# A hybrid decoder layer: the feed-forward stages' first chunk pair in seven products instead of eight

## The chip, the core and the metric

The program runs on one core of one Trainium2 chip. The time is device microseconds of one execution, from the start of the program to its end. Five engines work beside each other, each through its own list of instructions: PE (matrix multiply, with PEld for its weight loads), DVE (vector), ACT (scalar), POOL (GpSimd) and SP. SP computes nothing here: it issues the weight loads. POOL issues transfers too, among them the accumulating ones, which add what they read onto what stands in the on-chip memory.

## The reference

One decoder layer for 256 tokens of width 2048, in fp32: a SwiGLU feed-forward half step, a token mixer, another feed-forward half step, each followed by a layer norm of the sum with a scaled residual.

```python
def _swiglu(x, w_gate, w_up, w_down):
    return (jax.nn.silu(x @ w_gate) * (x @ w_up)) @ w_down

h = _layer_norm(ALPHA * h + 0.5 * _swiglu(h, ffn1_w_gate, ffn1_w_up, ffn1_w_down), ln1_g, ln1_b)
mix = _mixer(h, positions, ...)            # latent attention, differential attention, gates
h = _layer_norm(ALPHA * h + mix, ln2_g, ln2_b)
h = _layer_norm(ALPHA * h + 0.5 * _swiglu(h, ffn2_w_gate, ffn2_w_up, ffn2_w_down), ln3_g, ln3_b)
```

The feed-forward width is 5632. The change is about `x @ w_gate` and `x @ w_up`, in both feed-forward stages.

## The kernel before

**Tiles.** Tokens are two blocks of 128 (b = 0, 1). The width 2048 is 16 k tiles of 128, in four quads of four. Gate and up weights are stored interleaved, in 22 chunks of 512 columns (256 of gate, 256 of up). A chunk's weights come in eight pieces of two k tiles, 128x1024, half a megabyte each (`raw`, four buffers). A product is a matmul of 128 tokens with 128x512 weights.

**Splitting.** PE multiplies numbers in a short form (fp32r). So every operand is split into a high part (a cast on ACT, L154) and a low part (a subtraction on DVE, L155), and each product is three matmuls, high by high, high by low, low by high (`triple`, L208 to L210). The split weights go into a ring of six pairs (`wring`).

**Plain form and seven products.** `project` computes a chunk in plain form: 16 k tiles, two token blocks, three matmuls, 96 a chunk, 192 a pair of chunks. `Hybrid.group` takes a pair of chunks and multiplies part of the k tiles by a scheme with seven products in place of eight: the operands are blocks 11, 12, 21, 22 of weights (first or second chunk of the pair as the second figure, first or second half of the k tiles concerned as the first) and sums of them, and sums of x (`Seven`: `fa`, `fb`, `minus`, `as_is`, whose split forms are `xs`). In `wide` groups each of the seven products has five k tiles (the fifth comes from `Extra`, `xe`, `xm` and the half pieces `eraw`), and three of eight pieces a chunk stay plain: 7 x 15 + 72 = 177 matmuls a pair. A weight sum is formed in two ways: by DVE (block 22 added to 11, then 21 to 11, L451), or by POOL with an accumulating transfer of block 12 onto 11 and onto 22 (L453, L458). Product 5 needs 11 + 12, so it waits for the transfer that is issued once product 1 has split 11.

**Order.** A string gives the order of units: a digit is a product, `p` and `q` a plain piece of the first and second chunk, `n` the next pair's product 1. Units go through a pipeline of load, split and multiply, three and four units deep; `later(n, f)` runs f n units on. The instructions of each engine are then put in order at build time by a scheduler that counts on its own estimates of durations; `issue_after` holds an instruction behind another on the same engine. On the chip each engine follows its list. A load waits for its buffer, and SP's later loads stand behind it.

**A feed-forward stage before the change:** pair 0 by `project` twice (chunk 0, chunk 1, x being loaded or, in stage two, normalised meanwhile), then pairs 1 to 10 by `Hybrid`, pair 1 with its product 1 as the first unit and Y seeded only from pair 2 on. In stage two pair 1's blocks are loaded early, in `second`. Then comes the down projection, in which `setup` makes the mixer's constants (mask, biases, sines), 70 units after the layer norm object is made.

Of the kernel before, what the change touches and what calls it, by code (L numbers as in the profile page):

```python
# [59 lines left out]
def layer_kernel(ctx: ExitStack, tc: tile.TileContext, a: dict, out: bass.AP):  # L60
# [55 lines left out]
    class Acts:  # L116
        def __init__(self, k, name, kept=()):
            self.name = name
            self.kept = kept
            self.tiles = {}  # L120
            self.ready = set()
            self.made = {}
            self.cast = {}
            self.raws = {}
# [13 lines left out]
        def put(self, q, b, src, i0=0, n=4):  # L138
            hi, lo = self.quad(q, b)
# [126 lines left out]
    class Seven:  # L266


        def __init__(self, raws, order=None, plain=None):

            self.raws, self.order, self.plain = raws, order, plain
            self.at_ = {}
            self.steps = [self.sums, lambda: self.pair(self.fa, 5, 6), lambda: self.pair(self.fb, 7, 3),
                          self.as_is, self.minus]

# [80 lines left out]
    class Hybrid:  # L356


        def __init__(self, x, seven, k_tiles, small=False, extra=None, early=()):
# [3 lines left out]
            self.early = set(early)  # L363
            names = ("11", "12", "22", "21") if small else ("11", "22", "21", "other 11")
            self.raws = {n: early[n] if n in early else [act_tile([P, 1024], F32, "sraw") for _ in range(2)] for n in names}
            self.shared = False
            if extra is not None:
                for pair in (("11", "22"), ("21", "other 11")):
                    t = act_tile([P, 2, 512], F32, "eraw")
                    for i, n in enumerate(pair):  # L370
                        self.raws[n] = self.raws[n] + [t[:, i, :]]
            self.snaps = [act_tile([P, 2, 512], F32, "snap") for _ in range(2)]

# [4 lines left out]
        def run(self, groups):  # L378

            parts = []  # L380
            for g in groups:
                parts.append(self.group(*g[:-1]))
                self.raws["11"], self.raws["other 11"] = self.raws["other 11"], self.raws["11"]
            for i, (order, emit) in enumerate(parts):
                groups[i][-1]()
                for c in order if i == 0 else order[1:]:
                    if c != "n":
                        emit(c)
                    elif i + 1 < len(parts):
                        parts[i + 1][1]("1")  # L390

        def group(self, w0, w1, done, wide=False, seeded=False, gates=False):
# [4 lines left out]
            there, self.early = self.early, ()  # L397
# [37 lines left out]
            def seventh(p, s):  # L435
# [4 lines left out]
                def load():  # L440
                    if s < 2 and load_block in there:
                        return
                    nc.sync.dma_start(R[load_block][s], source(load_block, s))
# [256 lines left out]
    def rows_to_quad(src, b, x, q, gain=None, shift=None, shared=False):  # L700
# [3 lines left out]
        if gain is not None:  # L704
            full = x.raw(q, b) if q in x.kept else tmp_tile([P, 512], "full")
            if shared and q % 2 == 1:
                v, o = (u.rearrange("p (i t) -> p i t", i=4) for u in (full, t))
                g, b0 = (u[:, 4 * q:4 * q + 4].unsqueeze(2).to_broadcast([P, 4, P]) for u in (gain, shift))
                with tc.issue_after(x.made[q - 3, b].ins) if q > 2 else nullcontext():
                    V.tensor_tensor(out=v, in0=o, in1=g, op=ALU.mult)  # L710
# [60 lines left out]
    class LayerNorm:  # L771
# [109 lines left out]
        def apply(self, b):  # L881
# [42 lines left out]
            for c in range(4):  # L924
# [4 lines left out]
            for c in range(4):  # L929
                later((12 if self.ahead is None else 10 + 4 * b) + c, lambda c=c: self.each(b, c, zs[c]))  # L930

    def ffn(n, x, wgu, wdn, residual, g, bt, each, first=None, between=None, nxt=None, cols=None, norm=None, pending=None):
# [7 lines left out]
        def half(c, b, up, gate, wait=0, single=False):  # L940
            q = c // 2
            sg = tmp_tile([P, 256], "sg")
            with tc.issue_after(weights[0][0].ins) if single else nullcontext():
                S.activation(sg, gate, AF.Silu)
            if c % 2 == 0:
# [3 lines left out]
            def product():  # L949
                with tc.issue_after(weights[0][1].ins) if single else behind_split(3) if wait else nullcontext():  # L950
# [5 lines left out]
            if c % 2 == 1:  # L956
                later(12, lambda: put_h(b, q))

        def gu_done(c, b, bank):
            if c == 0:  # L960
                later(3, lambda: half(c, b, bank[:, 256:512], bank[:, 0:256], 1, True))
            else:
                half(c, b, bank[:, 256:512], bank[:, 0:256])

        def sum_done(c, b, bank, snap, op):
            if snap is None:
                gu_done(c, b, bank)
# [30 lines left out]
        early = {}  # L998

        def second(j):  # L1000
            if j == (6 if norm is None else 0):
# [3 lines left out]
            if norm is not None and j in (0, 2, 4):  # L1005
                name, w, j0 = (("11", 2, 0), ("22", 3, 2), ("21", 2, 2))[j // 2]
                early[name] = [act_tile([P, 1024], F32, "sraw") for _ in range(2)]
                for s in range(2):
                    nc.sync.dma_start(early[name][s], wgu[w][j0 + s])

        def first_hook(j):
            if first is not None:
                first(j)
            if j == 5:
                for i, f in enumerate([extra.make] + seven.steps):
                    later(2 * i + 1 - (i > 0), f)
# [5 lines left out]
        def ask():  # L1022
            for i, q in enumerate((3, 4, 0)):
                for b in range(2):
                    later(1 + 4 * i + 2 * b, lambda q=q, b=b: get_half(q, b))
            later(13, lambda: split_h(3))
            later(16, lambda: split_h(4))
        hy.run([(wgu[2 * p], wgu[2 * p + 1],
                 lambda n, b, bank, snap, op, p=p: sum_done(2 * p + n, b, bank, snap, op),
                 True, p > 1, ask if p == KF // 4 - 1 else lambda: None)  # L1030
                for p in range(1, KF // 4)])
# [3 lines left out]
        if n == 1:  # L1035
            later(70, setup)
# [444 lines left out]
    xq = Acts(KD, "x", (0, 1, 2))  # L1481
# [6 lines left out]
    def first_tokens(j):  # L1488
        if j % 2 == 0:
            load_x(j // 2, 0)  # L1490

    def second_tokens(j):
        if j % 2 == 0:
            load_x(j // 2, 1)
# [9 lines left out]
    ffn(1, xq, a["gu1"], a["dn1"], a["x"], a["ln1_g"], a["ln1_b"], keep(0), first_tokens, second_tokens, h1, a["ln1_cols"])  # L1504
# [3 lines left out]
    h2 = Acts(KD, "h2", (0, 1, 2))  # L1508
# [96 lines left out]
```

## Time and profile before

| | |
|---|---|
| median of 3 runs | 1982.29 us (1978.77 to 1983.79) |
| the profiled execution's own time | 1982.59 us |
| its span, first to last instruction | 1980.8 us |
| PE busy | 1960.7 us, 99% |
| DVE busy | 1743.7 us, 88% |
| ACT busy | 1269.4 us, 64% |
| granted TensorE clock, mean | 0.996 |

Rows of the views are read like this. A timeline row is start, duration, engine, line, operation, result<-operands, shape and count, in us from the span's start; a bracket behind it gives the engine's idle time before it and what ended that. A windows row is a stretch, its length, then busy time and instruction count of PE, PEld, DVE, ACT and POOL, the granted TensorE clock (1.00 is full), the busy share of the DMA engines and GB/s. A DMA row is the transfer, the queue's engine, count, size and median us from issue to landing. A matmul's duration of 0.39 us overlaps the next one's.

### The profile page before, as it was taken

The page shows a single profiled execution, that of the slowest core. Times are in us where ns is not written, and L with a number is a line of the kernel's source. Part 1 is how long each engine was busy: PE and PEld are TensorE (multiplying, and loading weights), DVE is VectorE, ACT ScalarE, POOL GpSimd, SP SyncE. Part 2 cuts the span into 40 slices and gives each one's busy share as a digit, 9 for nine tenths or more (in the row PEclk, how much of TensorE's full clock was granted, in tenths as well). Part 3 has the DMA queues.
Part 4 walks back from the last instruction along what each step waited for, and adds up shares of the span by engine and source line. Part 5 has one row for each costly group of instructions (what it writes and reads, how often), then busy time and mean ns, then how long its engine had stood idle before and what let it go on. Part 6 is the DMA issues. An engine that isn't in the chain of part 4 may idle for free. (4 is left out here: it accounts for less than half of the span.)

```text
span 1980.8 us, 25910 instructions
## 1 busy us (share of the span) xinstructions
PE 1960.7 (99%) x8751; PEld 1617.2 (82%) x8751; DVE 1743.7 (88%) x2161; ACT 1269.4 (64%) x1660; POOL 367.8 (19%) x600
## 2 busy tenths in 40 slices
PE   9899999999999999999999999999999999999998
PEld 8788888888878888888888888887888888888886
DVE  7799999999898879999987777779999999999997
ACT  6567766676656576666667655556767667766662
POOL 0112221222100010102241530011222123210000
PEclk9999999999999999999999999999999999999999
DMA  8888888787867657668686798688888878887773
GB/s 308 257 258 227 248 276 275 223 257 258 302 211 247 196 187 296 232 213 255 214 255 202 228 303 275 204 274 246 235 252 284 265 221 245 264 323 242 275 233 125
DMA packets 151958, 489.93 MB, mean 247 GB/s; under 512 B 21984, under 2 KB 22288, under 8 KB 151824
## 3 DMA queue, kind: packets, MB, share of 16 engines
q1 hardware_dynamic: 111744, 374.78, 53.4%
q0 software_dynamic: 39936, 113.35, 24.0%
q8 instruction: 68, 1.11, 0.2%
q14 instruction: 66, 0.54, 0.1%
q10 hardware_dynamic: 144, 0.13, 0.0%
HBM read 457.77 MB, written 30.41 MB: 246 GB/s over the span
## 5 line engine op out<-in xcount | busy, mean ns | idle before, releaser
L154 ACT CAST wring<-raw 128x1024 fp32r<-128x1024 f32 (+2 forms) x460 | 474.1, 1035 | 298.9 <-PE mm L210 211.7
L155 DVE TENSOR_TENSOR wring<-raw,wring 128x1024 fp32r<-128x1024 f32 (+2 forms) x460 | 545.4, 1198 | 111.0 <-ACT wring L154 108.7
L154 ACT CAST wring<-sraw 128x1024 fp32r<-128x1024 f32 x436 | 456.2, 1052 | 175.7 <-PE mm L210 67.4
L155 DVE TENSOR_TENSOR wring<-sraw,wring 128x1024 fp32r<-128x1024 f32 x436 | 524.5, 1217 | 47.8 <-ACT wring L154 43.7
L208 PE MATMUL mm<-wring,h 128*128 128x512 f32 (+2 forms) x1176 | 454.4, 386 | 0.0
L209 PE MATMUL mm<-wring,h 128*128 128x512 f32 (+2 forms) x1176 | 452.4, 385 | 0.4 <-DVE wring L155 0.4
L210 PE MATMUL mm<-wring,h 128*128 128x512 f32 (+2 forms) x1176 | 452.6, 385 | 0.0
L208 PEld LDWEIGHTS mm<-wring,h 128*128 128x128 f32 x1176 | 221.2, 188 | 47.0 <-ACT snap L409 3.3
L209 PEld LDWEIGHTS mm<-wring,h 128*128 128x128 f32 x1176 | 221.1, 188 | 44.1 <-DVE wring L155 1.1
L210 PEld LDWEIGHTS mm<-wring,h 128*128 128x128 f32 x1176 | 221.1, 188 | 43.8 <-DVE h L155 0.9
L209 PE MATMUL mm<-wring,xs 128*128 128x512 f32 x616 | 239.9, 390 | 0.2 <-DVE wring L155 0.2
L208 PE MATMUL mm<-wring,xs 128*128 128x512 f32 x616 | 240.1, 390 | 0.0
L210 PE MATMUL mm<-wring,xs 128*128 128x512 f32 x616 | 239.7, 389 | 0.0
L451 DVE TENSOR_TENSOR sraw<-sraw,sraw 128x1024 f32<-128x1024 f32 x128 | 153.7, 1217 | 1.2 <-DMA sraw<-in_wgm_dram 0.7
L209 PEld LDWEIGHTS mm<-wring,xs 128*128 128x128 f32 x616 | 115.7, 188 | 25.1 <-DVE wring L155 1.0
L210 PEld LDWEIGHTS mm<-wring,xs 128*128 128x128 f32 x616 | 115.6, 188 | 24.1
L208 PEld LDWEIGHTS mm<-wring,xs 128*128 128x128 f32 x616 | 115.6, 188 | 24.1
L749 POOL DMA_DIRECT2D hT<-blocks x176 | 98.4, 575 | 182.5 <-DVE blocks L747 94.8
L453 POOL DMA_DIRECT2D sraw<-in_gu_dram x40 | 35.1, 885 | 435.4 <-DVE sraw L451 410.5
L208 PE MATMUL mm<-wring,x 128*128 128x512 f32 x264 | 103.8, 396 | 0.4 <-ACT wring L154 0.4
L209 PE MATMUL mm<-wring,x 128*128 128x512 f32 x264 | 103.4, 392 | 0.2 <-DVE wring L155 0.2
L210 PE MATMUL mm<-wring,x 128*128 128x512 f32 x264 | 103.3, 391 | 0.0
(350 smaller groups left out, 2876.7 us busy)
## 6 DMA issues: line engine op xcount, KB each, us to landing
raw<-in_gu_dram SPq DMA_DIRECT2D x150, 512.0 KB, 6.3
raw<-in_dn_dram SPq DMA_DIRECT2D x140, 512.0 KB, 4.6
sraw<-in_gu_dram SPq DMA_DIRECT2D x120, 512.0 KB, 6.7
sraw<-in_gu_dram POOLq DMA_DIRECT2D x80, 512.0 KB, 7.0
sraw<-in_dn_dram SPq DMA_DIRECT2D x36, 512.0 KB, 5.7
raw<-in_w_out_dram SPq DMA_DIRECT2D x32, 512.0 KB, 4.4
eraw<-in_gu_dram SPq DMA_DIRECT2D x60, 256.0 KB, 6.9
hraw<-hT POOLq DMA_DIRECT2D x56, 256.0 KB, 5.1
```

The lines of the kernel that those rows point to most:

```text
L154: cast[0] = S.copy(hi, src)
L155: lows[0] = V.tensor_tensor(out=lo, in0=src, in1=hi.bitcast(F32), op=ALU.subtract)
L208: PE.matmul(o, xh, wh, start=first, stop=False, skip_group_check=again)
L209: PE.matmul(o, xh, wl, start=False, stop=False, skip_group_check=again)
L210: PE.matmul(o, xl, wh, start=False, stop=last, skip_group_check=again)
L451: last = V.tensor_tensor(out=R[src][i], in0=R[src][i], in1=R[add[1]][i], op=ALU.add)
L453: nc.gpsimd.dma_start(R["22"][s], source("12", s), accum_op=ALU.add)
L749: nc.gpsimd.dma_start(to.rearrange("(g r) (i f) -> i r g f", g=4, i=4)[i], t[32 * i:32 * (i + 1), :].rearrange("r (g f) -> r g f", g=4))
```

## The change

In both feed-forward stages pair 0 is computed by a new method, `Hybrid.opening`, with the order `pqp1qpqp536n2q74`. k tiles 0 to 7 go through the seven products with four k tiles each (no fifth), k tiles 8 to 15 stay plain, four pieces a chunk. Seven of the eight plain pieces are put in the order ahead of product 5. Products 1, 6 and 7 share a bank A in turn, product 5 has a bank D; their sums are kept in `snap` and added at the end. Product 1 of pair 1 stands inside the opening, at `n`, and pair 1 is seeded like the later ones.

Quads 0 and 1 of x (the `formed` ones) are no longer split as they are; they enter only in the forms. The quads are loaded, and in stage two normalised, in the order 2, 3, 0, 1. `run` now starts each group when it is reached. The early loads of pair 1's blocks in stage two are gone. `setup` is traced 84 units after the layer norm object instead of 70, which is 14 units further on. The layer norm's writes of its result to memory come earlier in the count of units.

```diff
+        def opening(self, w0, w1, done, order, hook, guard, settle):
+            plan = {1: ("11", "11", None, "A"), 5: (None, "11", None, "D"), 6: (None, "11", "22", "A"),
+                    7: (None, "22", None, "A"), 2: ("21", "21", None, "Y"), 4: (None, "11", "21", "W"),
+                    3: ("22", "22", None, "Z")}
...
+                def prep():
+                    t = block(src)[s]
+                    last = None
+                    if add is not None:
+                        with behind_split(s + 1):
+                            last = V.tensor_tensor(out=t, in0=t, in1=block(add)[s], op=ALU.add)
+                    pair = next_pair()
+                    with guard(u), tc.issue_after(last.ins) if last is not None else nullcontext():
+                        split_in_line(True, *pair, t)
+                    if p in (1, 6):
+                        nc.gpsimd.dma_start(block("11" if p == 1 else "22")[s], w1[s], accum_op=ALU.add)
...
+            def plain(u, n, j):
...
+                def prep():
+                    pair = next_pair()
+                    with guard(u):
+                        for c in parts:
+                            split_in_line(u > 8, *(t[:, c] for t in pair), st["raw"][:, c])
...
-        project(wgu[0], x, KD, 512, lambda b, bank: gu_done(0, b, bank), hook=first_hook,
-                between=between, norm=norm)
-        project(wgu[1], x, KD, 512, lambda b, bank: gu_done(1, b, bank), hook=second, norm=norm, free=(0, 0))
-        look(3, 4)
-        hy = Hybrid(x, seven, KD, extra=extra, early=early)
...
+            def begin():
+                if p == 0:
+                    return hy.opening(wgu[0], wgu[1], done, "pqp1qpqp536n2q74", first, guard, settle)
+                return hy.group(wgu[2 * p], wgu[2 * p + 1], done, True, True)
...
-            later(70, setup)
+            later(84, setup)
...
-    xq = Acts(KD, "x", (0, 1, 2))
+    xq = Acts(KD, "x", (0, 1, 2), (0, 1))
...
-    h2 = Acts(KD, "h2", (0, 1, 2))
+    h2 = Acts(KD, "h2", (0, 1, 2), (0, 1))
```

How this moves the instructions is seen in the engines' lists. The names: `raw` is a plain piece, `sraw` and `eraw` are block pieces, `xs` a split form of x, `sg` the gate's activation, `snap` a kept sum; DMAHW stands for a transfer that SP issued, DMASW for one of POOL's, mostly an accumulating one.

ACT, stage one, where product 5 is first cast. Before, this is pair 1's product 5 (sraw_83, sraw_84 and eraw_91 are block 11):

```order
L154 CAST wring_14_114<-raw_95_478 128x1024 [waits DMAHW2_49,DVE_49,PE_49]
L944 ACTIVATE sg_81_454<-mm_59_317 128x256 [waits PE_49]
L154 CAST wring_4_104<-sraw_83_463 128x1024 [waits DMASW0_49,DVE_49,PE_49]
L154 CAST wring_20_120<-eraw_91_471 128x512 [waits DMASW2_49,DVE_49,PE_49]
L944 ACTIVATE sg_98_508<-mm_60_324 128x256 [waits PE_49]
L154 CAST wring_2_102<-sraw_84_464 128x1024 [waits DMASW1_49]
```

Now it is pair 0's (sraw_36 and sraw_37 are block 11; raw_42, raw_41, raw_44 and raw_47 are plain pieces, in the order in which PE takes them):

```order
L158 CAST wring_20_120<-raw_42_222 128x1024 [waits DMAHW4_49,DVE_49,PE_49]
L158 CAST wring_14_114<-sraw_36_197 128x1024 [waits DMAHW5_49]
L158 CAST wring_4_104<-sraw_37_198 128x1024 [waits DMAHW6_49]
L158 CAST wring_14_114<-sraw_36_197 128x1024 [waits DMASW0_49,DVE_49,PE_49]
L158 CAST wring_2_102<-raw_41_219 128x1024 [waits DMAHW2_49]
L158 CAST wring_18_118<-raw_44_227 128x1024 [waits DMAHW1_49]
L158 CAST xs_48_244<-fa_45_232 128x1024 [waits DVE_49]
L158 CAST wring_16_116<-raw_47_238 128x1024 [waits DMAHW2_49]
L158 CAST wring_4_104<-sraw_37_198 128x1024 [waits DMASW1_49,PE_49,Activation_49]
```

Product 1's two casts and product 5's first follow one another, and three plain pieces' casts stand behind the latter.

SP, stage one, the loads behind the plain pieces (sraw_50 and sraw_51 are block 22, raw_68 is the last plain piece, raw_72 and raw_81 are pair 1's):

```order
L498 DMA raw_47_238<-in_gu1_dram 128x1024 [waits DMAHW2_49,DVE_49]
L498 DMA raw_68_391<-in_gu1_dram 128x1024 [waits DMAHW4_49,DMAHW3_49,DVE_49]
L626 DMA raw_72_436<-in_gu1_dram 128x1024 [waits DVE_49]
L461 DMA sraw_50_250<-in_gu1_dram 128x1024 [waits DMAHW5_49]
L626 DMA raw_81_489<-in_gu1_dram 128x1024 [waits DMAHW6_49,DMAHW1_49,DVE_49]
L461 DMA sraw_51_251<-in_gu1_dram 128x1024 [waits DMAHW7_49]
```

raw_68 takes the buffer of raw_41, so this load and those behind it wait for raw_41's split.

ACT, stage two, the same place (sraw_1507 and sraw_1508 are block 11, raw_1516 and raw_1519 the last plain pieces ahead of product 5; before, sraw_1540, sraw_1541 and eraw_1574 were pair 1's block 11). Before:

```order
L154 CAST wring_2_102<-raw_1578_10737 128x1024 [waits DMAHW7_49,DVE_49,PE_49]
L944 ACTIVATE sg_1570_10720<-mm_1543_10563 128x256 [waits DMASW6_49,DMASW7_49,DMASW0_49,PE_49]
L154 CAST wring_1462_10133<-sraw_1540_10555 128x1024 [waits DMASW6_49,DVE_49,PE_49]
L154 CAST wring_1458_10129<-eraw_1574_10732 128x512 [waits DMASW0_49,PE_49]
L944 ACTIVATE sg_1581_10767<-mm_1548_10591 128x256 [waits DMASW2_49,DMASW7_49,DMASW1_49,PE_49]
L154 CAST wring_1460_10131<-sraw_1541_10556 128x1024 [waits DMASW7_49,DVE_49]
```

Now:

```order
L317 ACTIVATE xs_1505_10428<-h2raw_1476_10292 128x512
L158 CAST wring_18_118<-raw_1516_10517 128x1024 [waits DMAHW3_49,PE_49]
L158 CAST wring_1447_10131<-sraw_1507_10442 128x1024 [waits DMAHW7_49]
L158 CAST wring_1449_10133<-raw_1519_10525 128x1024 [waits DMAHW4_49,PE_49]
L158 CAST wring_1445_10129<-sraw_1508_10443 128x1024 [waits DMAHW0_49]
L158 CAST wring_1447_10131<-sraw_1507_10442 128x1024 [waits DMASW2_49,DVE_49,PE_49]
L448 COPY snap_1511_10467<-tr_1509_10448 128x512 [waits PE_49]
L158 CAST wring_1445_10129<-sraw_1508_10443 128x1024 [waits DMASW3_49,DVE_49]
L158 CAST xs_1520_10527<-fa_1517_10519 128x1024 [waits DVE_49]
L158 CAST xs_1524_10538<-fb_1518_10520 128x1024 [waits DVE_49]
```

Product 5's two weight casts stand one instruction behind product 1's, and the casts of the forms of x that products 5 and 3 need stand behind them. The constants of `setup`, though traced 14 units on, keep their place on DVE between the same neighbours up to the product `lp`; only what follows it is shuffled.

More of the change, by code (lines that the diff above doesn't have):

```diff
@@ L378, in run @@
         def run(self, groups):
[L380 to L385, printed above, removed]
+            parts = [groups[0]]
+            for i, (start, ask) in enumerate(groups):
+                order, emit = parts[i] if i else start()
+                ask()
                 for c in order if i == 0 else order[1:]:
@@ L1004, in second @@
                 set_ring(6)
[L1005 to L1016, printed above, removed]
@@ L1032, in ffn @@
+        hy.run([pair_of(p) for p in range(KF // 4)])
         ln = LayerNorm(0.5, residual, g, bt, each, nxt, cols,
```

211 lines of the change are left out of this document (161 added, 50 removed).

## The prediction

> **What bounds the kernel now.** I read the page's busy shares first, then the stretches by engine, the timeline of PE where it has gaps, and there the timelines of ACT, POOL and SP.
>
> ```profile
> span 1980.8 us, 25910 instructions
> PE 1960.7 (99%) x8751; PEld 1617.2 (82%) x8751; DVE 1743.7 (88%) x2161; ACT 1269.4 (64%) x1660; POOL 367.8 (19%) x600
> ...
> 58.00:70.00 12.00, 6.98 (x17) 5.20 (x17) 8.07 (x9) 6.85 (x10) 0.04 (x1) 0.72 0.59 221
> ...
> 1400.00:1500.00 100.00, 100.00 (x440) 82.05 (x440) 92.86 (x105) 68.64 (x87) 20.92 (x31) 1.00 0.89 278
> ```
>
> PE is the bound, at 100/440 = 0.2273 us per 512-column matmul (1400 to 1500, a stretch without a gap). DVE is at 93% there, so it makes up little once it is late. 58 to 70 is the largest hole, and it follows the opening which the change rewrites:
>
> ```profile
> 57.72 0.39 PE L210 MATMUL tr<-wring,xs 128*128 128x512 f32 x1
> 62.38 0.51 PE L208 MATMUL tr<-wring,xs 128*128 128x512 f32 x1 [4.27 <-ACT wring L154]
> 63.64 0.79 PE L209 MATMUL tr<-wring,xs 128*128 128x512 f32 x1 [0.76 <-DVE wring L155]
> 64.23 0.63 PE L210 MATMUL tr<-wring,xs 128*128 128x512 f32 x1
> 64.66 0.63 PE L208 MATMUL tr<-wring,xs 128*128 128x512 f32 x1
> ...
> 70.04 0.40 PE L209 MATMUL mm<-wring,x 128*128 128x512 f32 x1
> ...
> 1339.99 0.39 PE L210 MATMUL tr<-wring,xs 128*128 128x512 f32 x1
> 1340.81 0.49 PE L208 MATMUL tr<-wring,xs 128*128 128x512 f32 x1 [0.43 <-ACT wring L154]
> 1342.06 0.50 PE L209 MATMUL tr<-wring,xs 128*128 128x512 f32 x1 [0.76 <-DVE wring L155]
> 1342.40 0.39 PE L210 MATMUL tr<-wring,xs 128*128 128x512 f32 x1
> ```
>
> From 57.72 to 70.04 there are 17 matmuls, 3.9 us at the usual pace, in 12.3: 8.5 lost. Some 3.4 of it is not waiting: the matmuls stand 0.43 apart, at half clock, for about 7 us after the wait. The second stage loses 1.7 at the same place (2.4 us for three steps). ACT shows what held PE:
>
> ```profile
> 54.05 1.05 ACT L154 CAST wring<-sraw 128x1024 fp32r<-128x1024 f32 x1 [5.73 <-PE mm L210]
> 60.49 0.62 ACT L154 CAST wring<-eraw 128x512 fp32r<-128x512 f32 x1 [5.38 <-DMA eraw<-in_gu_dram]
> 61.01 0.38 ACT L944 ACTIVATE sg<-mm 128x256 f32<-128x256 f32 x1
> 61.29 1.03 ACT L154 CAST wring<-sraw 128x1024 fp32r<-128x1024 f32 x1
> ...
> 44.12 1.03 POOL L458 DMA_DIRECT2D sraw<-in_gu_dram  x1 [42.01 <-DVE wring L155]
> ...
> 69.96 0.85 POOL L453 DMA_DIRECT2D sraw<-in_gu_dram  x1 [22.81 <-DVE sraw L451]
> ```
>
> ACT works strictly in its written order. The eraw cast waited 5.38 us for an accumulating DMA (POOL adds block 12 onto block 11 for product 5), and the sg behind it and the next sraw cast went only then. How late such a DMA is, by the issues of four short stretches (that of 44.12, the next half megabyte behind it, that of 69.96, and the first of stage two, at 1323.31):
>
> ```profile
> sraw<-in_gu_dram POOLq DMA_DIRECT2D x1, 512.0 KB, 9.8
> ...
> sraw<-in_gu_dram POOLq DMA_DIRECT2D x1, 512.0 KB, 12.4
> ...
> sraw<-in_gu_dram POOLq DMA_DIRECT2D x1, 512.0 KB, 5.5
> ...
> sraw<-in_gu_dram POOLq DMA_DIRECT2D x1, 512.0 KB, 9.0
> ```
>
> So 5.5 us with SP's queue empty, and 9 to 12.4 beside SP's loads.
>
> **The change, part by part.** Matmuls: a chunk pair costs 192 in plain form, 7 × 12 + 8 × 12 = 180 in the new one: 24 fewer over two stages, 24 × 0.2273 = 5.5 us off PE. That is the sure term. The rest is who waits. I compare one point: the opening pair and the next pair's product 1 are done. In the kernel before that is 192 + 15 = 207 matmuls, now 195. Before, 57.72 starts the 225th, so the 207th ends at 57.72 - 17 × 0.2273 = 53.9; with the 8.5 lost right behind it, which the old opening causes, **62.4** is to be beaten. Stage two: 1339.99 - 3.9 + 1.7 = **1337.8**.
>
> Stage one, new. The first 24 matmuls need the same bytes in the same sizes as before. Loads land in SP's order:
>
> ```profile
> 9.73 1.05 ACT L154 CAST wring<-raw 128x1024 fp32r<-128x1024 f32 x1 [0.69 <-DMA raw<-in_gu_dram]
> ...
> 14.32 0.62 ACT L154 CAST x<-xraw 128x512 fp32r<-128x512 f32 x1 [0.92 <-DMA xraw<-in_xT_dram]
> ...
> 10.82 1.22 DVE L155 TENSOR_TENSOR wring<-raw,wring 128x1024 fp32r<-128x1024 f32 x1 [1.05 <-ACT wring L154]
> ...
> 8.23 0.40 PE L208 MATMUL mm<-wring,x 128*128 128x512 f32 x1
> ...
> 1371.04 3.49 DVE L155 TENSOR_TENSOR wring<-raw,wring 128x1024 fp32r<-128x1024 f32 x3
> ```
>
> Eight quarter megabytes had landed at 9.73 and fifteen at 14.32: 0.656 us each. Block 11's first half is now the 18th: 9.73 + 10 × 0.656 = 16.3, cast and split (1.05 + 1.22) done at 18.6. Then POOL issues the accumulate. SP has some 2 MB under way until about 21.5, and its next load waits for a buffer, so I take 6.5 us, near the lower row: 25.1. ACT's order now has product 5's first cast, which waits for that DMA, ahead of the casts of the plain tiles that PE takes before product 5. PE's 61st matmul is the first of these. At 8.23 the 7th starts; 54 × 0.2273 make 20.5. Two plain tiles on the way come late: the third (11 quarters: 11.7, split done at 14.0, wanted at 12.7) costs 1.3, the fourth (16 quarters: 15.0, done 17.3, wanted 16.8) 0.5. So 22.3. The cast is ready at 25.1 + 2 × 1.05 = 27.2, its low part 1.2 later: PE is held about 5 us, 5.6 with that step.
>
> Behind it DVE has, to product 4's last split, 24 instructions of 128x1024 (3.49 / 3 = 1.16 each), 5 of half that size and two small ones, 31.4 us; PE 135 matmuls, 30.7, and 3.4 more if the clock halves as it did after 4.27 us. From 28.4 that gives, with the last five matmuls, 60.9 by DVE and **62.5** by PE. The later wins: 62.5, +0.1. With 5.5 us and no slow clock 59.4 (-3.0), with 9.8 us 65.8 (+3.4).
>
> [...]
>
> Stage two, new. PE's opening begins at 1339.99 - 224 × 0.2273 less 2.2 for 16 transposes = 1286.9.
>
> ```profile
> 1277.50 0.69 DVE L871 BATCH_NORM_STATS2 bn<-z 128x6 f32<-128x512 f32 x1
> ...
> 1279.60 1.91 DVE L925 TENSOR_SCALAR z<-z,mv,f 128x512 f32<-128x512 f32 x4
> ...
> 1289.05 0.68 DVE L866 TENSOR_TENSOR z<-mm,z 128x512 f32<-128x512 f32 x1
> ...
> 1280.91 1.50 ACT L715 ACTIVATE h2raw<-tr,cols 128x128 f32<-128x128 f32 x4 [1.06 <-PE tr L703]
> ...
> 47.99 1.09 SPq L443 DMA_DIRECT2D sraw<-in_gu_dram  x2
> ...
> 49.67 0.96 SPq L443 DMA_DIRECT2D sraw<-in_gu_dram  x2
> ```
>
> Token block 1's last sum at 1289.05, its statistics to the first normalised quarter 2.1 + 0.6, transposes 0.5: ACT can go on at 1292.8, with 8 gains (1.50 per four), two casts, the minus and two weight casts (6.7 us) up to product 1's; its split ends at about 1301.0 and the second half's, two splits on, at 1303.3. These are the two issues. SP, freed by the same splits at 1300 and 1302, then sends six sraw and four eraw loads, 4 MB, where 47.99 to 51 sent 2.5. So here the upper rows are nearer: 9.0 and, queued behind it, 10.5, so the second lands at 1313.8 (bounds: 5.5 and one transfer behind, 1309.1; 12.4, 1315.7). Product 5's own left-hand form (xs, from fa) stands on ACT behind **both** waiting casts: 1313.8 + 2.0 = 1315.8. PE arrives there after 92 matmuls and the transposes at 1310.5 and waits 5.3 us. DVE is idle meanwhile and then has 21 long, 5 middle and 2 small instructions to product 4, 27.9, and PE five matmuls more: **1344.8**, +7.0. Bounds +2.3 and +8.9.
>
> [...]
>
> In both stages ACT also has a cast for the **next** pair's product 5 (its accumulate is issued some 9 us earlier) ahead of product 4's casts. At 7 to 9 us to landing that costs nothing, at 12.4 about 3. I take 1 each, 0 to 3.
>
> At nothing: fewer x splits (quadrants 0 and 1 get none: 4 casts and 4 subtractions a stage) run on engines that wait anyway; pair two's Y bank is seeded, one DVE subtraction less. The mixer's constants are traced 14 units later, but DVE's order round them is unchanged up to lp, so the wait inside them stays:
>
> ```profile
> 589.76 0.51 PE L208 MATMUL tr<-wring,xs 128*128 128x512 f32 x1
> 592.09 0.80 PE L209 MATMUL tr<-wring,xs 128*128 128x512 f32 x1 [1.82 <-DVE wring L155]
> ...
> 595.59 0.40 PE L208 MATMUL mm<-wring,h 128*128 128x512 f32 x1
> ```
>
> It would be worth 3.8 if it went: these are nine steps, 2.05 us at the usual pace, in 5.83.
>
> Sum: 1982.6 of the profiled execution (0.3 above the median) + 0.1 + 7.0 + 2 = 1991.7, the gain of 5.5 being inside the 195. Against it stands pair two's lighter DVE: I say **1991**.
>
> **The rivals.** (1) The accumulates land early, 5.5 us each: the casts hold ACT briefly, stage one -3.0, stage two +2.3, no second hold: 1982, no change. For it: the early one in stage one has a quiet queue. Against: none beside a busy SP queue took under 9.0 here, and stage two is at +2.3 even so. (2) Faster: ACT's order does not bind, because DVE's and PE's backlog at those places is longer than I count. Then the 5.5, the 8.5 and the 1.7 are all won and 1.8 at the start lost: 13.9, or 1969; half of it 1976. For it: before, stage two's DMA took 9.0 us too and PE lost only 1.7, since PE had plain tiles to eat. Against: now the plain tiles are first, and their casts (stage one) or the form (stage two) stand behind the wait. (3) Slower still: the transfer times are those after 44.12 in both stages and the second hold takes 3: +3.4 + 8.9 + 6 = 2001. It decides where SP's loads are under way when POOL issues. (4) The constants do move off DVE's busy stretch: 3.8 less than any of these.
>
> **How the numbers follow.** Forecast 0.42, rival (3) 0.12, rival (1) 0.27, rival (2) 0.19; (4) is spread in them. A measurement here can tell 0.3%, 6 us, from no change: slower 0.54, no change 0.27, faster 0.19. The forecast's own range is 1987 to 1997. The range with 2 in 10 outside is cut into rival (2) at its half, 1975, and ends at 1999, where rival (3) begins.
>
> **What would show it.** PE waits of 4 to 6 us at its 61st matmul, released by ACT, with half clock behind; in stage two a wait of about 5 us some 24 us after the output projection, released by ACT, ACT itself idle on a DMA of sraw; the hole at 58 gone. 24 matmuls fewer. Wrong, if ACT shows no idle time on sraw in either opening, if PE's first 60 us have no gap over 2 us, or if DVE stays busy through both.

## The result, and the profile after

| | before | changed |
|---|---|---|
| median | 1981.26 us, 4 runs (1978.77 to 1983.79) | 2005.0 us, 4 runs (2003.36 to 2006.25) |
| ratio to before, 95% interval | | 1.012 (1.0106 to 1.0133) |
| the profiled execution's own time | 1982.59 us | 2005.7 us |

Slower, as forecast, but by 24 us and not by 9: 2005.0 lies above the range (1975 to 1999). The page of the changed kernel, and PE's longest waits in it (total, times, longest):

```profile
span 2003.9 us, 25920 instructions
...
PE 1964.4 (98%) x8727; PEld 1611.9 (80%) x8727; DVE 1768.0 (88%) x2183; ACT 1279.6 (64%) x1672; POOL 374.4 (19%) x608
...
PE tr L212 <- ACT xs L158: 9.2, 1, 9.2
PE mm L213 <- DVE wring L159: 7.7, 13, 1.3
PE mm L212 <- ACT wring L158: 4.9, 3, 4.4
```

PE has 24 matmuls fewer (8751 to 8727). The wait of 4.27 us at 62 is gone too. In its place stand one of 4.4 us and one of 9.2, both released by ACT, and 13 short ones on DVE (3 before, 0.8 us in all).

**Where the 23.1 us between the two profiled executions are.** Both kernels do the same before and behind an opening, so I take as one measure the time to the start of the last matmul of the opening and the next pair together, counted in 512-column matmuls: the 384th before, the 372nd now. PE's timeline has these starts, before (stage one's 384th, stage two's first and 384th):

```profile
102.53 0.39 PE L210 MATMUL mm<-wring,x 128*128 128x512 f32 x1
...
1287.07 0.39 PE L208 MATMUL mm<-wring,h 128*128 128x512 f32 x1
...
1378.97 0.39 PE L210 MATMUL mm<-wring,h 128*128 128x512 f32 x1
```

and in the changed kernel (the 195th, which is the forecast's point, and the 372nd of stage one; the first, the 195th and the 372nd of stage two):

```profile
62.70 0.39 PE L212 MATMUL mm<-wring,xs 128*128 128x512 f32 x1
106.89 0.39 PE L214 MATMUL mm<-wring,x 128*128 128x512 f32 x1
1293.19 0.39 PE L212 MATMUL mm<-wring,h 128*128 128x512 f32 x1
1358.37 0.40 PE L214 MATMUL mm<-wring,xs 128*128 128x512 f32 x1
1402.21 0.39 PE L214 MATMUL mm<-wring,h 128*128 128x512 f32 x1
```

Stage one ends 4.4 us later (106.89 against 102.53). Stage two takes 109.0 us from its first matmul in place of 91.9: 17.1 more. The stretch between the two stages takes 1186.3 in place of 1184.5: 1.8 more. That is 23.3; the rest, -0.2, is spread behind.

**Stage one's opening** went nearly as forecast. ACT, POOL and PE in the timeline:

```profile
24.43 1.04 ACT L158 CAST wring<-sraw 128x1024 fp32r<-128x1024 f32 x1 [6.51 <-DMA sraw<-in_gu_dram]
25.38 1.99 ACT L158 CAST wring<-raw 128x1024 fp32r<-128x1024 f32 x2
...
18.18 1.02 POOL L473 DMA_DIRECT2D sraw<-in_gu_dram  x1 [16.06 <-DVE wring L159]
...
26.47 1.22 PE L212 MATMUL mm<-wring,x 128*128 128x512 f32 x2 [4.44 <-ACT wring L158]
...
28.32 0.63 PE L214 MATMUL mm<-wring,x 128*128 128x512 f32 x1
```

POOL issued at 18.2, ACT sat on product 5's cast until 24.4, and PE's 61st matmul came at 26.47, after a plain piece's cast that stood behind it. Half clock followed (a matmul in 0.63, a granted clock of 0.50 from 26.4 to 31.4 us), until 31.3. The hold stopped SP as well: it issued no load between 17.0 and 27.7 us. The load that stood there is raw_72's, which needs the buffer of raw_41, unsplit behind the hold; raw_68's had gone at 16.7, as soon as raw_42 was split.

**Stage two's opening** is where the forecast fell short:

```profile
1305.37 1.05 ACT L158 CAST wring<-raw 128x1024 fp32r<-128x1024 f32 x1 [2.37 <-PE mm L214]
...
1320.24 1.04 ACT L158 CAST wring<-sraw 128x1024 fp32r<-128x1024 f32 x1 [10.98 <-DMA sraw<-in_gu_dram]
...
1324.00 1.04 ACT L158 CAST wring<-sraw 128x1024 fp32r<-128x1024 f32 x1 [2.23 <-DMA sraw<-in_gu_dram]
1324.95 1.04 ACT L158 CAST xs<-fa 128x1024 fp32r<-128x1024 f32 x1
...
1332.72 0.59 ACT L448 COPY snap<-tr 128x512 f32<-128x512 f32 x1 [4.12 <-PE tr L214]
...
1310.18 0.89 POOL L473 DMA_DIRECT2D sraw<-in_gu_dram  x1 [9.78 <-DVE wring L159]
1311.64 0.86 POOL L473 DMA_DIRECT2D sraw<-in_gu_dram  x1 [0.57 <-DVE wring L159]
...
1326.04 0.80 PE L212 MATMUL tr<-wring,xs 128*128 128x512 f32 x1 [9.17 <-ACT xs L158]
1326.63 0.63 PE L213 MATMUL tr<-wring,xs 128*128 128x512 f32 x1
```

The accumulating transfers were issued at 1310.2 and 1311.6 and their data was cast at 1320.2 and 1324.0. The form of x that PE needed stood behind both casts. When PE went on, it did so at half clock (0.51 granted from 1326 to 1332 us), and ACT's next copy then waited 4.12 us for PE.

**Behind the openings** PE does not come back to its pace in the next pair. The stretches from the 195th to the 372nd matmul (columns as explained for the windows rows):

```profile
62.70:106.89 44.19, 41.96 (x179) 32.79 (x177) 42.93 (x50) 28.38 (x39) 9.76 (x14) 1.00 0.81 235
1358.37:1402.21 43.84, 41.67 (x179) 32.83 (x177) 42.56 (x50) 28.62 (x39) 9.71 (x14) 1.00 0.82 238
...
106.89:147.22 40.33, 40.33 (x178) 33.15 (x177) 37.61 (x43) 28.07 (x36) 9.65 (x14) 1.00 0.90 277
```

The last row is the next 177 matmuls of stage one. In the kernel before, the 177 behind its 207th are these, in both stages:

```profile
53.64:102.53 48.89, 43.87 (x178) 35.09 (x177) 40.12 (x45) 31.08 (x40) 9.76 (x14) 0.93 0.89 267
1335.91:1378.97 43.06, 41.66 (x178) 32.84 (x177) 38.61 (x44) 29.47 (x38) 9.70 (x14) 1.00 0.83 245
```

177 matmuls are 40.2 us at the usual pace and take 44.2 and 43.8, at full clock. DVE is busy for 42.9 and 42.6 of them. In the steady stretch before, 440 matmuls went with 92.86 us of DVE, so 177 with 37.4. In this pair DVE has some 5 us more to do: it still owes what belongs to the opening and already makes what the following pair needs. By number, 49 of its instructions start in this stretch and 42 in each later one: four of the seven more are splits for the following pair, three end the opening's sums. In the kernel before, the four were there too; DVE's work came to 40.1 and 38.6 us, just under PE's 40.3, and now it is over it.

### The profile page after: what moved, and what is told of

Its sections match the earlier page's. It is cut to its first block, busy times and chain, and to the rows that moved or that the text cites. A ratio compares the mean times of both kernels' runs of the same rounds, so it can differ in the third digit from the quotient of the medians.

```text
span 2003.9 us, 25920 instructions
## 1 busy us (share of the span) xinstructions
PE 1964.4 (98%) x8727; PEld 1611.9 (80%) x8727; DVE 1768.0 (88%) x2183; ACT 1279.6 (64%) x1672; POOL 374.4 (19%) x608
## 4 chain that ended last, share of the span: by engine, by line
PE 85%; DVE 5%; DMA 4%; issue 3%; ACT 2%; POOL 0%; SPq 0%; DVEq 0%; ACTq 0%; POOLq 0%
PE mm L213 24%; PE mm L212 24%; PE mm L214 24%; PE tr L213 4%; PE tr L214 4%; PE tr L212 4%; DVE wring L159 2%; DMA sraw<-in_gu_dram 2%; ACT wring L158 1%; DMA hraw<-hT 1%; DVE sraw L795 1%; DMA z<-in_x_dram 0%; PE tr L847 0%; DMA raw<-in_wgd_dram 0%; PE tr L1551 0%
## 5 line engine op out<-in xcount | busy, mean ns | idle before, releaser
L158 ACT CAST wring<-raw 128x1024 fp32r<-128x1024 f32 (+2 forms) x444 | 457.4, 1035 | 298.4 <-PE mm L214 212.2
L159 DVE TENSOR_TENSOR wring<-raw,wring 128x1024 fp32r<-128x1024 f32 (+2 forms) x444 | 525.8, 1196 | 113.1 <-ACT wring L158 110.0
L158 ACT CAST wring<-sraw 128x1024 fp32r<-128x1024 f32 x464 | 483.9, 1051 | 202.0 <-PE mm L214 60.1
L159 DVE TENSOR_TENSOR wring<-sraw,wring 128x1024 fp32r<-128x1024 f32 x464 | 557.1, 1216 | 52.9 <-ACT wring L158 49.1
L212 PE MATMUL mm<-wring,h 128*128 128x512 f32 (+2 forms) x1144 | 442.0, 387 | 0.0
L213 PE MATMUL mm<-wring,h 128*128 128x512 f32 (+2 forms) x1144 | 440.3, 385 | 1.3 <-DVE wring L159 1.3
L214 PE MATMUL mm<-wring,h 128*128 128x512 f32 (+2 forms) x1144 | 440.6, 385 | 0.0
L213 PE MATMUL mm<-wring,xs 128*128 128x512 f32 x640 | 250.4, 391 | 5.4 <-DVE wring L159 5.3
L212 PEld LDWEIGHTS mm<-wring,h 128*128 128x128 f32 x1144 | 215.4, 188 | 45.7 <-ACT snap L555 2.9
L212 PE MATMUL mm<-wring,xs 128*128 128x512 f32 x640 | 250.2, 391 | 0.3 <-ACT wring L158 0.3
L213 PEld LDWEIGHTS mm<-wring,h 128*128 128x128 f32 x1144 | 215.4, 188 | 43.6 <-DVE wring L159 1.8
L214 PEld LDWEIGHTS mm<-wring,h 128*128 128x128 f32 x1144 | 215.5, 188 | 42.7 <-DVE h L159 0.5
L214 PE MATMUL mm<-wring,xs 128*128 128x512 f32 x640 | 249.2, 389 | 0.0
L213 PEld LDWEIGHTS mm<-wring,xs 128*128 128x128 f32 x640 | 120.1, 188 | 34.2 <-DVE wring L159 9.5
L212 PEld LDWEIGHTS mm<-wring,xs 128*128 128x128 f32 x640 | 120.1, 188 | 28.0 <-ACT wring L158 3.4
L214 PEld LDWEIGHTS mm<-wring,xs 128*128 128x128 f32 x640 | 120.2, 188 | 24.7
L212 PE MATMUL tr<-wring,xs 128*128 128x512 f32 x264 | 104.8, 397 | 11.6 <-ACT xs L158 9.2
L213 PE MATMUL tr<-wring,xs 128*128 128x512 f32 x264 | 104.1, 394 | 3.9 <-DVE wring L159 3.9
L214 PE MATMUL tr<-wring,xs 128*128 128x512 f32 x264 | 103.7, 393 | 0.0
```

The lines of the kernel that those rows point to most:

```text
L158: cast[0] = S.copy(hi, src)
L159: lows[0] = V.tensor_tensor(out=lo, in0=src, in1=hi.bitcast(F32), op=ALU.subtract)
L212: PE.matmul(o, xh, wh, start=first, stop=False, skip_group_check=again)
L213: PE.matmul(o, xh, wl, start=False, stop=False, skip_group_check=again)
L214: PE.matmul(o, xl, wh, start=False, stop=last, skip_group_check=again)
```

## The experiments

"Stage one" and "stage two" in the tables are the measure above, each from the one profiled execution. That one can lie off the median: in the first three runs below by -4.4, +3.4 and +3.6 us. Stage one counts from the start of the span, and its first matmul stands anywhere from 5.2 to 6.2 us; two pairs of runs with the same code there differ by 0.8 and 1.3 us, so a difference of 1 us in that column says little. "Run" is the median. Its ratio, with the interval, is to the kernel before as measured beside that run (medians 1979.2 to 1980.5).

### Without the accumulating transfer, and with product 5's casts later

```diff
-                    if p in (1, 6):
-                        nc.gpsimd.dma_start(block("11" if p == 1 else "22")[s], w1[s], accum_op=ALU.add)
+                    if p == 6:
+                        nc.gpsimd.dma_start(block("22")[s], w1[s], accum_op=ALU.add)
```

> Left out: the two transfers in each opening that add block 12 onto block 11, so product 5 and what is built on it are computed from other weights; the instructions of ACT, DVE and PE are the same and stand in nearly the same order. Theory A (the hold: ACT's cast for product 5 waits for that transfer, and the casts behind it wait with it): the 4.4 us and the 9.2 us of PE waiting go, with the half clock behind them (about 2.5 us each) and some of the short waits after: 2005 less 16 to 22, 1983 to 1989. Rival B (DVE is short of time in the opening and would hold PE as long anyway): less than 6 us goes, 1999 or more.

The second leaves all work in and changes only ACT's order:

```diff
+                    with ExitStack() as held:
+                        for i in [casts[-1]] + forms if p == 5 else []:
+                            held.enter_context(tc.issue_after(i.ins))
                         split_in_line(True, *pair, t)
```

> The same instructions and the same transfers; on ACT, product 5's two weight casts stand behind the casts of the plain pieces (stage one) and of the forms of x (stage two) instead of ahead of them. Theory A: stage one loses the 4.4 us wait and its half clock, 6 to 7 us; in stage two product 5's weights still land at 10 and 14 us after product 1's split, and PE's wait is 5 to 6 us in place of 9.2, 3 to 4 us less: 1994 to 1997. Rival C (not the order on ACT, but the late transfer itself, decides in both stages): 2002 to 2005. Rival B (DVE's debt): 2002 or more.

| | run | ratio | stage one | stage two |
|---|---|---|---|---|
| before | 1981.26 | | 102.5 | 91.9 |
| changed | 2005.0 | 1.012 (1.0106 to 1.0133) | 106.9 | 109.0 |
| no accumulating transfer | 1992.82 | 1.006 (1.0038 to 1.0082) | 105.5 | 96.9 |
| casts later | 1994.53 | 1.0072 (1.0051 to 1.0092) | 103.9 | 103.2 |

Both theories missed the first run: A wanted 1983 to 1989, B 1999 or more. The second run is in theory A's range. In stage two, taking the transfer away gave back 12.1 of 17.1 us. In stage one it gave 1.4 (2.4 counted from the first matmul). ACT's and PE's timelines without the transfer say why:

```profile
19.94 1.99 ACT L158 CAST wring<-sraw 128x1024 fp32r<-128x1024 f32 x2 [3.40 <-PE tr L214]
...
21.98 0.51 PE L212 MATMUL tr<-wring,xs 128*128 128x512 f32 x1 [1.40 <-ACT wring L158]
```

Product 5's cast still stood early on ACT, now ahead of product 1's second cast, and waited there for PE to free a pair of the ring. So in stage one it is the place of that cast that costs, whatever it waits for. The second run agrees: with the cast later, the wait of 4.4 us at the 61st matmul was gone (it started at 22.3 instead of 26.47). Yet only 3.0 us of the 6 to 7 that I expected came back by the 372nd. Stage two gave 5.8, where I expected 3 to 4; what was left of its wait shows here (ACT, PE, and the window with the granted clock at 0.51):

```profile
1317.99 1.04 ACT L158 CAST wring<-sraw 128x1024 fp32r<-128x1024 f32 x1 [4.77 <-DMA sraw<-in_gu_dram]
...
1319.09 0.49 PE L212 MATMUL tr<-wring,xs 128*128 128x512 f32 x1 [3.15 <-ACT wring L158]
...
1320.00:1330.00 10.00, 9.13 (x20) 6.42 (x21) 7.41 (x9) 6.96 (x9) 0.86 (x2) 0.51 0.71 279
```

So the hold on ACT is shown: its place in the order is worth about 10 us of the 24, and 12 go when the transfer goes too. The other half, and the 5.5 us and 10.2 us that should have been won, were still missing. That is what the next runs are about.

### The addition on DVE, and block 12 early

```diff
-            blocks = {"11": (w0, 0), "21": (w0, 2), "22": (w1, 2)}
-            plan = {..., 5: (None, "11", None, "D"), ...
+            blocks = {"11": (w0, 0), "12": (w1, 0), "21": (w0, 2), "22": (w1, 2)}
+            plan = {..., 5: ("12", "11", "12", "D"), ...
```

> Block 12 comes by a load of SP into a buffer of its own, and DVE adds it onto block 11; the accumulating transfer for product 5 is gone from both openings, for four more 128x1024 additions on DVE (4 x 1.2 us). Theory A: near the run without the transfer, less what DVE's additions cost, 1985 to 1994. Rival B: DVE is the bound in the opening, so the additions come on top: 2007 to 2010.

1994.36 us, 1.0072 (1.0051 to 1.0093), just above theory A's range and far from rival B's; stage one 107.0, stage two 99.9. Then, in stage two alone, the loads of block 12 were issued with block 11's:

```diff
-                    w, j0 = blocks[load_block]
-                    nc.sync.dma_start(block(load_block)[s], w[j0 + s])
+                    for n in [load_block] + (["12"] if p == 1 and hook is None else []):
+                        w, j0 = blocks[n]
+                        nc.sync.dma_start(block(n)[s], w[j0 + s])
```

> As the run with the addition on DVE (1994.4), but in stage two the loads of block 12 are issued right behind block 11's, ahead of the next pair's plain pieces, so that nothing is late at product 5. From the stage's first matmul to the end of the next pair took 99.9 us there, 96.9 without any addition, 91.9 before. Rival L (late transfers): 95 to 97 us, 1989 to 1992 in all. Theory D (DVE's work): 99 to 101 us, 1993 to 1996.

1993.71 us, 1.0072 (1.0057 to 1.0087), stage two 100.0: no gain from the earlier data, as theory D expected. There was little to gain: with the addition on DVE, ACT had waited only 0.4 us for a transfer in stage two. What both runs show is that with no transfer late at product 5, stage two is still 8 us above before.

### DVE relieved: four sums left out, and forms on POOL

```diff
-                    if add is not None:
-                        with behind_split(s + 1):
-                            last = V.tensor_tensor(out=t, in0=t, in1=block(add)[s], op=ALU.add)
```

> The order on ACT of the run before last (product 5's casts behind the plain casts and the forms), and in each opening DVE's four 128x1024 sums for products 6 and 4 left out, 4.6 us of DVE a stage, so these two products are computed from other weights. Theory D (DVE's debt: with the hold gone, DVE has as much work as PE from the opening through the next pair, so each us of DVE shows): 6 to 10 us less than 1994.5, 1984 to 1989. Rival L (late transfers and the way from cast to split to matmul bind, not DVE's sum of work): 1991 to 1995.

1990.41 us, 1.0048 (1.0033 to 1.0063): 4.1 less than with the casts later, for 9.3 us of DVE taken out. Stage one 102.5 (1.4 less), stage two 97.6 (5.7 less, of which about 2 is half clock that was shorter: 4 matmuls stand 0.43 apart, and 15 in the other run). This lies between the two expectations: less than half of DVE's work comes back as time, so DVE's sum is a part of the rest and not all of it. The pair behind the opening, in which DVE keeps its 49 instructions, went from 44.2 and 43.8 us to 42.8 and 42.6. In the other runs of the changed kernel it took 44.2 to 45.4 and 43.4 to 43.9, whatever was changed in the opening; only with PE kept busy (below) it took 42.5 in stage two.

```diff
-                V.tensor_tensor(out=out, in0=in0, in1=in1, op=ALU.subtract)
+                nc.gpsimd.tensor_tensor(out=out, in0=in0, in1=in1, op=ALU.subtract)
```

> The same order on ACT; the eight subtractions that form the sums of x (fa, fb: 4 of 128x512, 0.60 us each; fe: 4 of 128x128, 0.2 us each) go from DVE to POOL in every stage that has them, 3.2 us of DVE for an opening. Theory D: 3 to 6 us less than 1994.5, 1988 to 1992. Rival L: 1993 to 1996. POOL's own time for these is in no run so far; if it is several times DVE's, the forms are late in stage two and the run is above 1996.

1999.31 us, 1.0095 (1.0079 to 1.0112), slower: in number the last case of the expectation. POOL takes 1.3 to 2.2 us for a form where DVE takes 0.68 (0.60 from one start to the next), and its transfer stands among them:

```profile
20.67 1.49 POOL L294 TENSOR_TENSOR fb<-xraw 128x512 f32<-128x512 f32 x1
21.90 1.10 POOL L478 DMA_DIRECT2D sraw<-in_gu_dram  x1
```

Both stages took 1 us longer than with the casts later (104.9 and 104.1). The rest of the 4.8 us between the medians was not traced, and that the forms were late is not shown.

### Another order, and a longer ring

> The same order on ACT; the opening runs pqp1qpq3p56n2q74: product 3 and a plain piece stand ahead of product 5, so the accumulating transfer has some 24 matmuls, 5.5 us, more. Rival L: the waits at product 5 in stage two (3.2 us and half clock) go, 5 to 8 us less than 1994.5, 1987 to 1990. Theory D: DVE's work is the same, only its order changes, 1992 to 1996.

Only the order string differs (`pqp1qpq3p56n2q74`). 1993.34 us, 1.0062 (1.0047 to 1.0077); stage one 104.0, stage two 101.0. Theory D's range. In stage two PE's longest wait for a cast of weights fell from 3.15 to 1.6 us and half clock from 15 matmuls to 8, and the stage got only 2.3 us shorter: product 5 later on PE is no cure.

```diff
-                set_ring(6)
+                set_ring(7)
```

> The run with product 5's casts later (1994.5), with a ring of seven pairs of split weights in place of six, so that a cast finds its pair free one unit earlier. Rival L (the way from cast to split to matmul through the ring, casts that wait for PE): 3 to 6 us less, 1988 to 1992. Theory D (DVE's sum of work from the opening through the next pair): the ring changes nothing once DVE is full, 1993 to 1996.

1991.92 us, 1.006 (1.0045 to 1.0075). The median is in rival L's range, but not for its reason: stage one took 108.2, 4.3 more, stage two 101.9, 1.4 less, and the stretch between them 1179.9, 7.5 less. The ring does not shorten the two stages together. Some 4 of the 7.5 lie in the down projection, where the wait of 1.82 us and the half clock behind it are missing. They are missing too in the kernel before with seven pairs (below), but also in the run without the transfer, with six (from 585 to 600 us no wait over 0.81 us, and a granted clock of 1.00), so the ring is not shown to be the cause.

### The price of the slow clock

```diff
+                    if p == 5 and s == 0 and hook is None:
+                        full = self.x.tiles[1, 0][0]
+                        for _ in range(36):
+                            with tc.issue_after(newest[0].ins):
+                                newest[0] = PE.matmul(o, full[:, 0, :], full[:, 4:8, :].rearrange("p k t -> p (k t)"),
+                                                      start=True, stop=True, skip_group_check=True)
```

> The changed kernel, with 36 more 512-column matmuls of no use (8.2 us) on PE where it stands 9.2 us in stage two, ahead of product 5's first; the bank that they write is reset by product 5. Theory A with the clock: PE's gap is 1 us or less, the 13 matmuls behind it run at 0.23 us in place of 0.43, and the stage is 2 to 3 us shorter: 2002 to 2003. If the slow clock costs nothing, since DVE sets the end of the opening anyway (theory D): 2004 to 2006.

2000.84 us, 1.0102 (1.0085 to 1.0119): 4 less than the changed kernel, where 2 to 3 were expected. PE's timeline:

```profile
1317.47 8.32 PE L486 MATMUL tr<-h 128*128 128x512 f32 x36
...
1327.13 0.50 PE L214 MATMUL tr<-wring,xs 128*128 128x512 f32 x1 [1.33 <-ACT xs L158]
1327.46 0.40 PE L215 MATMUL tr<-wring,xs 128*128 128x512 f32 x1
```

Product 5's first matmul starts as late after the stage's first (32.8 us, 32.9 without them), but at full clock (1.00 granted from 1320 to 1340 us). Stage two, with the idle matmuls not counted, is 104.4, 4.6 less. Half clock is 2.6 of that (13 matmuls, 0.43 against 0.23 apart). The other 2 may come from ACT's copy of product 5's bank, which no longer waits 4.12 us for a slow PE; but the build also put that copy five casts later, so this part is not separated.

### The constants, alone

```diff
-            later(84, setup)
+            later(70, setup)
```

> Only the mixer's constants go back to 70 units after the layer norm object. If their place matters as little as DVE's order says (same neighbours up to lp): 2003 to 2007. If moving them is part of the loss, the 1.3 us that the down projection lost come back and more: 2000 to 2003. If the move gained something: 2008 or more.

2005.04 us, 1.0124 (1.0104 to 1.0144); stages 107.7 and 108.8. Moving the constants does nothing that can be measured.

### The kernel before, with one pair of casts exchanged

```diff
-                    with tc.issue_after(last.ins) if last is not None and not small else nullcontext():
+                    with tc.issue_after(last.ins) if last is not None and not small else nullcontext(), \
+                            tc.issue_after(cast[0].ins) if p == 5 and s > 0 and not small else nullcontext():
                         split_in_line(not small, *pair, t)
```

> The kernel before, with one thing changed: on ACT, product 5's second cast (whose transfer was issued second) stands ahead of its half piece's cast (issued third), as PE wants them, and not behind it. Theory A (PE stood 4.27 us at 62 because that cast queued behind the last transfer): the second transfer lands 1 to 3 us ahead of the third, 2 to 6 us less, 1975 to 1979. If the two land together, 1979 to 1982.

1976.63 us (10 runs), 0.9982 (0.9972 to 0.9991): faster than the kernel before and the changed one. ACT and PE where the hole of 4.27 us was:

```profile
58.19 1.04 ACT L154 CAST wring<-sraw 128x1024 fp32r<-128x1024 f32 x1 [2.40 <-DMA sraw<-in_gu_dram]
60.86 0.62 ACT L154 CAST wring<-eraw 128x512 fp32r<-128x512 f32 x1 [1.62 <-DMA eraw<-in_gu_dram]
...
59.29 0.49 PE L208 MATMUL tr<-wring,xs 128*128 128x512 f32 x1 [0.95 <-ACT wring L154]
```

The second block's transfer had landed 2.7 us ahead of the half piece's, and PE waits 0.95 us in place of 4.27. Stage one is 99.2, 3.3 less. The ring of seven on top of it:

> The kernel before with product 5's casts in PE's order (1976.6), and the ring of seven pairs. DVE has idle time there in the plain pair (12 of 20 us between 40 and 60), which a longer ring would let it use: 1972 to 1976. If what holds DVE there is the blocks' buffers and not the ring: 1976 to 1978.

1978.05 us (10 runs), 0.9989 (0.9979 to 0.9999): no better. Between 40 and 60 us DVE worked 7.2 us with seven pairs and 8.2 with six, so it is not the ring that keeps DVE from working ahead in the plain pair. The time itself says less: in stage one (102.8) PE now waited 4.0 us at 69.7 for a copy on ACT, which it did not with six.

## Why the prediction was right and wrong

**The mechanism was right, and in stage one's opening the size came out too, in part by luck.** POOL's issue (forecast 18.6, measured 18.2), the landing (25.1, 24.4), the held matmul (the 61st), its wait (about 5, 4.44) and the end of the opening (62.5, 62.70) stand as the prediction had them. The hole at 58 went, as it said. But from the held matmul's low part on (27.73; forecast 28.4) half clock cost 2.0 us where the forecast has 3.4, and short waits and slow single steps took 2.9 that it does not have.

**The first step that failed: "I take 1 each, 0 to 3" for what comes behind the opening.** I followed DVE's list only to product 4's last split and then let PE run at its pace, with 1 us for the next pair's product 5. Against 62.4 and 40.1 us in the kernel before (102.53 - 62.4), stage one has +0.3 in the opening and +4.1 behind it (44.2). Stage two has 43.8 there, against 41.2 before (from 1337.8 to 1378.97): +2.6. The second hold of ACT, which this term was meant for, came in stage one alone, and ahead of the 195th matmul. It is ACT's cast for the next pair's product 5, whose transfer POOL issued at 47.7:

```profile
55.63 1.06 ACT L158 CAST wring<-sraw 128x1024 fp32r<-128x1024 f32 x1 [1.82 <-DMA sraw<-in_gu_dram]
```

Behind the 195th matmul ACT waited for no transfer, and DVE was full (42.9 of 44.2 us). The bound of 60.9 that I worked out "by DVE" was 1.6 us under the one by PE. That should have said that DVE leaves the opening with nothing in hand. The reference point was too hard as well: charging all 8.5 us of the old hole to the old opening assumes that the pair behind it runs at full pace otherwise. With the casts exchanged the hole's wait fell to 0.95 us, and the kernel before still took 45.3 and 42.9 us for these 177 matmuls. So no run shows that the 8.5 could all be won.

**The second: stage two's +7.0.** Measured from 1337.8 in the time of that stage it was +14.5. (a) The wait was 9.2 us, not 5.3. The issues came 17.0 and 18.5 us after the stage's first matmul, where I had 14.1 and 16.4, since the plain cast ahead of product 1's waited 2.37 us for a pair of the ring. The second transfer then took 12.4 us to its cast, the upper of my rows, where I took 10.5. (b) I charged half clock in stage one and not in stage two: 2.6 us, and with what hangs on it up to the 4.6 of the run with PE kept busy. From the wait's end to the 195th matmul 29.0 us were forecast and 32.3 measured.

**The sum.** 0.3 + 4.1 + 14.5 + 2.6 + 1.8 between the stages - 0.2 = 23.1, against 0.1 + 1 + 7.0 + 1 less a little. Of the miss of about 14, 7.5 are stage two's opening, 4.7 the pairs behind the openings, 1.8 the stretch between.

**The rivals.** (2), ACT's order does not bind, fell: moving product 5's casts gave 10 us. (3), slower still by the rows after 44.12, was nearest in stage two (+8.9, with the 12.4 us that came), but it too had the pairs behind at 6 for another reason. (1) fell: product 5's four transfers landed 6.2 and 7.3 us after their issue in stage one, 10.0 and 12.3 in stage two, and none in 5.5. (4) stayed away, and the constants alone changed nothing.

**What stays open.** Without hold or late transfer the new openings were still 12 to 15 us above before in all. DVE's work is part of that, as the sums left out show. Most of the rest is in the openings themselves: in the run with block 12 early they take 55.3 and 56.2 us from the first matmul to the 195th, some 11 more each than the usual pace; before, 207 matmuls took 48.0 and 48.8. Where that goes, on the way from cast to split to matmul, was not separated; neither the other order, nor the longer ring, nor earlier data removed it. One rival was not tested by itself, the loads in stage one: from 20 to 60 us the DMA engines are busy for 0.96 of the time in the changed kernel, 0.91 before. Against it, ACT waited 8.7 us for transfers there with product 5's casts later and 2.8 with the addition on DVE and block 12 early, and stage one was not shorter for that (103.9 and 105.7).

## What to carry to other kernels

A plain stretch at the start is not only slow work: the engine that prepares has time to spare in it. Here DVE worked 25.7 us of the 40 between 20 and 60 us before, and 32.0 in the changed kernel, which had more to make up behind it. Before taking matmuls out of it, compare preparation and multiplication through the following stretch as well, not just to the end of what is changed. And on an engine that works in order, as ACT did here (two plain casts went right behind the one that had waited 6.51 us), look where an instruction that waits for a late transfer stands: two casts exchanged in the old kernel took 3.2 us off, while 24 matmuls fewer, with the waits that came with them, added 24.

## What the runs showed of the hardware

**Half clock came behind a wait of 1.82 us too, shorter than the 4.27 us of the kernel before, and not every time.** The wait of 1.82 us in the down projection stands in the timelines of eight profiled executions; half clock followed in six, right behind it or within 1.2 us, and not in two. It followed in the kernel before (0.63 a matmul from 592.68, the nine steps of 5.83 us) and not in the same kernel with the casts exchanged:

```profile
587.93 0.51 PE L209 MATMUL tr<-wring,xs 128*128 128x512 f32 x1 [1.82 <-DVE wring L155]
588.28 0.39 PE L210 MATMUL tr<-wring,xs 128*128 128x512 f32 x1
```

The stretch between the two stages varied from 1179.9 to 1187.6 us over the profiled executions, of which this is one cause (some 1.7 us). What decides whether the clock falls behind such a wait is not shown.

**With useless matmuls in the wait the clock stayed up**: with 36 of them where PE had waited 9.2 us, the granted clock was 1.00 from 1320 to 1340 us; without them, 13 matmuls behind the wait ran at half clock, 0.43 us apart.

**POOL took 1.3 to 2.2 us** for a 128x512 subtraction, in the run with the forms on POOL; DVE took 0.68.
